# Expert weights loaded as 8 KB runs, and the latents' expert products of the first layer cut into 32-column tiles

## The chip, the cores and the metric

The kernel runs on one core of one Trainium2 chip. The metric is the device time of one launch in microseconds (us), as the median over several runs. The profile is one execution of the same program, recorded instruction by instruction. Engines are named as in the profile: PE (matrix multiply), PEld (its weight load), DVE (vector), ACT (scalar), POOL (GpSimd), SP (the queue that issues most transfers).

## The reference, cut to what matters

The program is two transformer blocks after each other, each of two layers, on 512 latent tokens of width 1024; the second block also carries 256 context tokens. The change touches only the mixture of experts that ends each layer of the second block. In layer 0 it runs on the context and on the latents, in layer 1 on the latents alone.

```python
def ec_moe(h, w_router, w_gate, w_up, w_down):
    bsz, n_tok, d = h.shape
    cap = EC_CAPACITY * n_tok // N_EXPERTS
    aff = jax.nn.softmax(jnp.einsum('bnd,de->bne', h, w_router).astype(jnp.float32), axis=-1)
    g, idx = lax.top_k(jnp.swapaxes(aff, 1, 2), cap)
    xs = jax.vmap(lambda hb, ib: hb[ib])(h, idx)
    hid = jax.nn.silu(jnp.einsum('becd,edf->becf', xs, w_gate)) * jnp.einsum('becd,edf->becf', xs, w_up)
    ye = jnp.einsum('becf,efd->becd', hid, w_down) * g[..., None].astype(h.dtype)
    return jax.vmap(lambda yb, ib: jnp.zeros((n_tok, d), h.dtype).at[ib.reshape(-1)].add(yb.reshape(-1, d)))(ye, idx)
```

There are 16 experts; each takes 64 latent tokens and 32 context tokens (`cap`). Its three weight matrices are 1024 x 1024 in fp32, 4 MB each, so a layer's experts are 192 MB. `h` is the layer-normed token, scaled and shifted by two rows of the conditioning vector (`adaln`).

## The kernel before

`moe(l, lat, ctx_)` works in groups. In layer 0 (`two` is true) there are four groups of four experts, in layer 1 eight groups of two. A group has blocks of 128 gathered token rows: in layer 0 one context block (four experts of 32 tokens) and two latent blocks (two experts of 64 tokens), in layer 1 one latent block. `gather` fetches the rows, transposes them on PE (`tr` into `ptm`; the rows are `q` in the profile) and writes `xT`, with the scale and shift applied on DVE and ACT.

A product has the tokens as the stationary operand (`xT` or `hid`, 32 or 64 columns) and the weights as the moving one, 512 columns at a time. `tile_position=(0, c0)` puts each expert's tokens into their own columns of the array, so that four matmuls of 32 columns, or two of 64, run at the same time. We call four (or two) such neighbours a set. Each fp32 matmul of the program is two recorded instructions, so a set is passed twice. Accumulators are `pm` (six PSUM banks), evacuated by silu on ACT (gate) and a multiply on DVE (up). The product is transposed again into `hid` (two `ptm` banks), and `w_down` is applied. `Columns.down` scales by the router's weight. In all but the last group of layer 0 the rows then go to memory by indirect adds on POOL (`acc`). Elsewhere a one-hot matrix (`sel`) adds them into the rows kept on chip (`Columns.spread`).

`wload` fetches weights in pieces of 1 MB into rotating slots: 14 in layer 0, 18 in layer 1. A piece is one expert's 512 rows by 512 columns, so a run in memory is 512 columns, 2 KB. The last group's `w_down` of layer 1 uses pieces of 256 columns (1 KB runs). One `product` covers 512 columns; gate, up, gate, up, down, down is the order within a group. Within a product the order `every` goes row by row of the contraction (k) over all blocks; `one_by_one` does one block after the other.

A scheduler decides the final order on each engine. SP issues loads in order, and a load waits for the last matmul that read its slot. In layer 1 the 16th to 18th load are issued by POOL (`LATE`).

Of the kernel before, what the change touches and what calls it, by code (L numbers as in the profile page):

```python
# [8 lines left out]
F32 = mybir.dt.float32  # L9
# [4 lines left out]
AF = mybir.ActivationFunctionType  # L14
# [72 lines left out]
def _build(tc, nc, st, a, out):  # L87
# [59 lines left out]
    def pj():  # L147
        return cur["ps"].tile([128, 512], F32, tag="j", name="pj", bufs=2)
# [10 lines left out]
    def tr(o, i):  # L159
        T.transpose(o, i, ident[: i.shape[0], : i.shape[0]])  # L160
# [14 lines left out]
    with tc.tile_pool(name="vl", bufs=1) as vl:  # L175
# [4 lines left out]
        o = 0  # L180
# [47 lines left out]
    def pin(ins, yes=True):  # L228

        return tc.keep_in_program_order(ins) if yes else ins  # L230
# [170 lines left out]
    z_d = [dr.tile([S, D], F32, name=f"z{l}") for l in range(NL)]  # L401
    mod_d = [dr.tile([2, 6 * D], F32, name=f"mod{l}") for l in range(NL)]
    modc = [con.tile([128, 96], F32, name=f"modc{l}") for l in range(NL)]
    cT = con.tile([128, 8, 32], F32, name="cT")

    def cond():
# [7 lines left out]
    def adaln(l, pool):  # L414

        mr = pool.tile([128, 12, 128], F32, tag="mr", name="mr")
        G.memset(mr, 0.0)
        for g in range(4):
            nc.sync.dma_start(mr[32 * g:32 * g + 2, :, :], bass.AP(
                a["b_mod_2"].tensor, a["b_mod_2"].offset + l * 6 * D + 128 * g, [[0, 2], [512, 12], [1, 128]]))  # L420
        for u in range(12):
            p = pj()
            for kq in range(4):
                w = wraw(a["w_mod_2"][l], 2 * kq, 2, 512 * u, 512)
                for k in range(2):
# [12 lines left out]
        V.tensor_copy(modc[l], p[:, :96])  # L438
        for c in range(2):
            for sc in (1, 4):  # L440
                s0 = 48 * c + 8 * sc
                V.tensor_scalar(modc[l][:, s0:s0 + 8], modc[l][:, s0:s0 + 8], 1.0, None, op0=OP.add)

    def mc(l, c, chunk, k):
        o_ = 48 * c + 8 * chunk + k
        return modc[l][:, o_:o_ + 1]
# [656 lines left out]
    def moe(l, lat, ctx_):  # L1103
# [17 lines left out]
        def pm():  # L1121
            return psm.tile([128, 512], F32, tag="m", name="pm", bufs=6)

        def wload(src, e, c0, n, kh):
            turn[0] = (turn[0] + 1) % len(order_)
            pool = order_[turn[0]]
            w = pool.tile([128, 4, 512], F32, tag="w", name="w", bufs=slots[id(pool)])

            late = len(order_) - LATE[l] <= loads[0] < len(order_)
            loads[0] += 1  # L1130
            w = w[:, :, :n]
            pin((nc.gpsimd if late else nc.sync).dma_start(w, src[l, e, 512 * kh:512 * kh + 512, c0:c0 + n].rearrange(
                "(k p) c -> p k c", p=128)), late)
            return w

        gms = {}
# [14 lines left out]
        def gather(s, i):  # L1151

            r = row4()
            pin(G.indirect_dma_start(out=r, out_offset=None, in_=s["rows"][:],
                                 in_offset=bass.IndirectOffsetOnAxis(ap=s["idx"][:, i:i + 1], axis=0)),
                loads[0] < 20)
            xT = xt(s["nm"])
            for kk in range(2):
                p = ptm()
                for k in range(4):  # L1160
                    tr(p[:, 128 * k:128 * k + 128], r[:, 512 * kk + 128 * k:512 * kk + 128 * k + 128])
                for k in range(4):
                    k_ = 4 * kk + k
                    o, i_, g, b = xT[:, k_, :], p[:, 128 * k:128 * k + 128], mc(l, s["c"], 4, k_), mc(l, s["c"], 3, k_)
                    if k % 2:
                        A.activation(o, i_, AF.Identity, bias=b, scale=g)
                    else:
                        V.tensor_scalar(o, i_, g, b, op0=OP.mult, op1=OP.add)  # L1168
            return xT

        def half_tile():
            return small([128, S], "ty", bufs=4)

        def group(i):
# [10 lines left out]
                blocks = [blocks[1], blocks[0], blocks[2]]  # L1185
            exps = [e for p_ in pairs for e in (p_, p_ + 8)]

            def product(src, cols, lhs, order):

                c, n = cols  # L1190
                if order is every:
                    ws = {(e, kh): wload(src, e, c, n, kh) for kh in range(2) for e in exps}
                else:
                    ws = {(e, kh): wload(src, e, c, n, kh) for p_ in pairs for kh in range(2) for e in (p_, p_ + 8)}
                outs = [pm() for _ in blocks]
                for step in order:
                    if callable(step):
                        step(outs)
                        continue
                    bs, ks = step  # L1200
                    for k in ks:
                        for bi in bs:
                            for e, c0, m in blocks[bi][1]:
                                mm(outs[bi][c0:c0 + m, :n], lhs[bi][:, k, c0:c0 + m], ws[e, k // 4][:, k % 4, :],
                                   k == 0, k == 7, tile_position=(0, c0))
                return outs

            all_k = range(8)
# [1 line left out]
            one_by_one = [([b], all_k) for b in range(len(blocks))]  # L1210
            hid = [mB.tile([128, 8, 128], F32, tag=f"hid{j}", name="hid", bufs=1) if two else
                   row4().rearrange("p (a b) -> p a b", b=128) for j in range(len(blocks))]
            for half in range(2):
                order = one_by_one if i == 0 and half == 0 else every
                gp = product(a["w_gate_2"], (512 * half, 512), [b[0] for b in blocks], order)
                gs = []
                for g in gp:
                    x = half_tile()
                    A.activation(x, g, AF.Silu)  # L1219
                    gs.append(x)  # L1220
                up = product(a["w_up_2"], (512 * half, 512), [b[0] for b in blocks], order)
                for bi, u in enumerate(up):
                    V.tensor_tensor(out=gs[bi], in0=u, in1=gs[bi], op=OP.mult)  # L1223
                    p = ptm()
                    for k in range(4):
                        tr(p[:, 128 * k:128 * k + 128], gs[bi][:, 128 * k:128 * k + 128])
                    copy(hid[bi][:, 4 * half:4 * half + 4, :].rearrange("p a b -> p (a b)"), p)

            if i == 0:
                late_rows()  # L1230
# [78 lines left out]
                    self.seen.add(nm)  # L1309

            waiting = None
            for c, n in ((0, 256), (256, 256), (512, 256), (768, 256)) if final and not two else ((0, 512), (512, 512)):
                x = Columns(c, n)
                if final and two:
                    product(a["w_down_2"], (c, n), hid, [
                        ([0], all_k), lambda dp: x.down(0, dp), ([1, 2], range(4)), ([1], range(4, 8)),
                        lambda dp: x.down(1, dp), lambda dp: x.spread(0), ([2], range(4, 6)), lambda dp: x.spread(1),
                        ([2], range(6, 8)), lambda dp: x.down(2, dp), lambda dp: x.spread(2)])
                    continue
                dp = product(a["w_down_2"], (c, n), hid, one_by_one if final else every)  # L1320
# [445 lines left out]
```

## Time and profile before

| What | Value |
|---|---|
| Median of three runs | 2866.74 us (2864.62 to 2875.64) |
| The profiled execution's own time | 2861.59 us |
| Its span, first to last instruction | 2859.8 us |
| PE busy, share of the span | 2483.4 us, 87% |
| Moved by DMA | 612.94 MB, 214 GB/s over the span |

The table is to be read with care: the shares are means over stages that have different limits. Experts of layer 0 run from about 1298 to 1939 us of the span, those of layer 1 from about 2338 us to the end.

### The profile page before, as it was taken

The page shows a single profiled execution, that of the slowest core. Times are in us where ns is not written, and L with a number is a line of the kernel's source. Part 1 is how long each engine was busy: PE and PEld are TensorE (multiplying, and loading weights), DVE is VectorE, ACT ScalarE, POOL GpSimd, SP SyncE. Part 2 cuts the span into 40 slices and gives each one's busy share as a digit, 9 for nine tenths or more (in the row PEclk, how much of TensorE's full clock was granted, in tenths as well). Part 3 has the DMA queues.
Part 4 walks back from the last instruction along what each step waited for, and adds up shares of the span by engine and source line. Part 5 has one row for each costly group of instructions (what it writes and reads, how often), then busy time and mean ns, then how long its engine had stood idle before and what let it go on. Part 6 is the DMA issues. An engine that isn't in the chain of part 4 may idle for free.

```text
span 2859.8 us, 36332 instructions
## 1 busy us (share of the span) xinstructions
PE 2483.4 (87%) x14703; PEld 1412.3 (49%) x14703; DVE 1228.3 (43%) x2361; ACT 802.2 (28%) x1522; POOL 504.6 (18%) x389
## 2 busy tenths in 40 slices
PE   7988898998998878968999999995898869877886
PEld 5755676665687566753222222234677733323233
DVE  5423554335649968762010101028678641212113
ACT  3362323353335436521000000004247320000001
POOL 2111312012223332331010101004223320000001
PEclk9999999999999988988999999997999979999998
DMA  5364553346433141169999998963221479999997
GB/s 183 104 195 126 163 146 110 123 131 186 143 112 132 55 152 36 45 232 326 342 354 340 330 355 297 340 234 104 66 66 37 147 267 387 387 387 387 387 387 272
DMA packets 354191, 612.94 MB, mean 214 GB/s; under 512 B 37585, under 2 KB 110823, under 8 KB 354023
## 3 DMA queue, kind: packets, MB, share of 16 engines
q1 hardware_dynamic: 344214, 576.71, 58.4%
q0 software_dynamic: 5824, 20.45, 2.3%
q10 hardware_dynamic: 3984, 13.45, 1.2%
q8 instruction: 116, 1.90, 0.3%
q14 instruction: 53, 0.43, 0.0%
HBM read 581.88 MB, written 28.67 MB: 213 GB/s over the span
## 4 chain that ended last, share of the span: by engine, by line
PE 39%; DVE 11%; DMA 9%; issue 7%; ACT 3%; POOL 2%; SPq 0%; DVEq 0%; POOLq 0%; ACTq 0%
PE pm L151 24%; PE pj L151 6%; DMA w<-in_w_up_dram 5%; PE pa L151 5%; DMA w<-in_w_down_dram 3%; DVE acc L850 2%; PE pt L151 2%; PE pt L160 1%; DVE wl L331 1%; PE ptm L160 1%; POOL lnst L249 1%; DVE s L245 1%; ACT P L456 1%; DVE Q L1609 0%; DVE ng L453 0%
## 5 line engine op out<-in xcount | busy, mean ns | idle before, releaser
L151 PE MATMUL pm<-w,q 128*64 128x512 f32 (+1 forms) x1600 | 368.9, 583 | 56.2 <-DMA w<-in_w_up_dram 23.0
L151 PE MATMUL pm<-w,xT 128*64 128x512 f32 (+1 forms) x2048 | 389.4, 607 | 0.4 <-DVE xT L1168 0.3
L151 PEld LDWEIGHTS pm<-w,q 128*64 128x64 f32 x1600 | 124.8, 137 | 276.5 <-issue 174.7
L329 ACT ACTIVATE wh<-w 128x1024 fp32r<-128x1024 f32 (+2 forms) x154 | 161.0, 1050 | 303.4 <-PE pj L151 103.4
L1223 DVE TENSOR_TENSOR ty<-pm,ty 128x512 f32<-128x512 f32 x40 | 27.6, 691 | 502.9 <-PE pm L151 502.9
L151 PEld LDWEIGHTS pm<-w,xT 128*64 128x64 f32 (+1 forms) x2048 | 90.5, 123 | 281.1 <-issue 264.7
L151 PE MATMUL pj<-hTh,wh 128*128 128x512 f32 x512 | 214.4, 420 | 12.2 <-ACT ty L301 6.4
L331 POOL TENSOR_TENSOR wl<-w,wh 128x1024 fp32r<-128x1024 f32 (+1 forms) x57 | 142.4, 2500 | 436.6 <-ACT wh L329 403.9
L151 PE MATMUL pm<-w,hid 128*64 128x512 f32 (+1 forms) x1024 | 210.7, 604 | 0.0
L151 PE MATMUL pj<-hTl,wh 128*128 128x512 f32 x512 | 207.7, 406 | 0.0
L151 PE MATMUL pj<-hTh,wl 128*128 128x512 f32 x512 | 205.1, 404 | 0.0
L331 DVE TENSOR_TENSOR wl<-w,wh 128x1024 fp32r<-128x1024 f32 (+2 forms) x97 | 136.3, 1405 | 104.0 <-ACT wh L329 103.6
L160 PE MATMUL pt<-ident,P 128*128 128x128 f32 x712 | 120.5, 289 | 11.2 <-DVE mx L133 3.1
L151 PE MATMUL pa<-wh,hTh 128*128 128x512 f32 x256 | 106.2, 416 | 23.2 <-DVE ty L948 15.1
L151 PEld LDWEIGHTS pm<-w,hid 128*64 128x64 f32 (+1 forms) x1024 | 47.1, 122 | 154.6 <-issue 152.2
L151 PEld LDWEIGHTS pj<-hTh,wh 128*128 128x128 f32 x512 | 100.2, 196 | 38.9 <-issue 8.1
L1219 ACT ACTIVATE ty<-pm 128x512 f32<-128x512 f32 x40 | 23.9, 597 | 314.6 <-PE pm L151 314.6
L151 PEld LDWEIGHTS pj<-hTl,wh 128*128 128x128 f32 x512 | 99.8, 195 | 24.1 <-issue 3.9
L151 PEld LDWEIGHTS pj<-hTh,wl 128*128 128x128 f32 x512 | 98.7, 193 | 24.4 <-issue 2.2
L135 DVE TENSOR_SCALAR P<-P,rc 128x256 f32<-128x256 f32 (+6 forms) x176 | 107.8, 635 | 4.4
L453 DVE TENSOR_REDUCE ng<-pa 128x1 f32<-128x513 f32 (+5 forms) x124 | 93.3, 756 | 36.9 <-PE pa L151 35.0
L151 PE MATMUL pa<-wh,hTl 128*128 128x512 f32 x256 | 104.4, 412 | 1.1 <-DVE hTl L370 1.1
(441 smaller groups left out, 4332.7 us busy)
## 6 DMA issues: line engine op xcount, KB each, us to landing
w<-in_w_gate_dram SPq DMA_DIRECT2D x128, 1024.0 KB
w<-in_w_up_dram SPq DMA_DIRECT2D x127, 1024.0 KB
w<-in_w_down_dram SPq DMA_DIRECT2D x118, 1024.0 KB
w<-in_w_mod_dram SPq DMA_DIRECT2D x96, 512.0 KB
w<-in_w_in_dram SPq DMA_DIRECT2D x94, 512.0 KB
w<-in_w_out_dram SPq DMA_DIRECT2D x40, 512.0 KB
w<-in_w_down_dram SPq DMA_DIRECT2D x16, 512.0 KB
z<-q ACTq DMA_DIRECT2D x8, 512.0 KB
```

The lines of the kernel that those rows point to most:

```text
L135: (G if eng == "g" else V).tensor_scalar(o, i, scale, None, op0=OP.mult)
L151: return T.matmul(o, l, r, start=start, stop=stop_, skip_group_check=True, **kw)
L160: T.transpose(o, i, ident[: i.shape[0], : i.shape[0]])
L245: pin(V.bn_stats(s6[:, c, :], x[:, c * w:c * w + w]))
L249: pin(G.tensor_tensor(out=rs, in0=ve, in1=mhalf[:, :n], op=OP.pow))
L329: A.activation(hi, w, AF.Copy)
L331: (lo_eng or (G if lot[0] % 3 == 0 else V)).tensor_tensor(out=lo, in0=w, in1=hi.bitcast(F32), op=OP.subtract)
L453: V.tensor_reduce(ng, S_[:, :, lo:hi], axis=AX, op=OP.max, negate=True)
L456: A.activation(P[:, i, lo:hi], S_[:, i, lo:hi], AF.Exp, bias=ng[:, i:i + 1], accum_out=su[:, i:i + 1])
L850: V.scalar_tensor_tensor(acc[:, c, :n], glu[:, c, tap:tap + n], w, acc[:, c, :n], op0=OP.mult, op1=OP.add)
L1219: A.activation(x, g, AF.Silu)
L1223: V.tensor_tensor(out=gs[bi], in0=u, in1=gs[bi], op=OP.mult)
```

## The change

Gate and up of every group, and down of all but each layer's last group, use a new function `wide`, with a new loader `wwide`. A piece is again 1 MB, but it is 256 rows by all 1024 columns. Partition p reads rows 4p+m (m is 0, 1 or 2, 3) of one half of the matrix, two neighbouring rows, so one run is 8 KB. Both column halves of a product accumulate at the same time: two `pm` banks for each block, all six in layer 0. Since a partition now holds rows 4p+m, the transposes that make `xT` and `hid` take every fourth column (`wide_rows`). For the same reason scale and shift are fetched in that order into `modw` (two more small transfers and eight small transposes per layer in `adaln`). Silu's output is kept in one `t4` tile per block in layer 0. In layer 0 the latents' blocks are cut into four tiles of 32 columns, two for each expert, in all products. The first group's gate does three quarters of the context block before the latents. The last group's down keeps its old loads.

```diff
+    def wide_rows(x, k):
+        return x[:, 512 * (k // 4):512 * (k // 4) + 512].rearrange("p (j m) -> p m j", m=4)[:, k % 4, :]
...
+        def wwide(src, e, j):
+            w = wslot().rearrange("p (k c) -> p k c", k=2)
             late = len(order_) - LATE[l] <= loads[0] < len(order_)
             loads[0] += 1
+            m = 2 * (j % 2)
+            pin((nc.gpsimd if late else nc.sync).dma_start(
+                w, src[l, e].rearrange("(h p m) c -> p h m c", h=2, m=4)[:, j // 2, m:m + 2, :]), late)
             return w
...
-                    tr(p[:, 128 * k:128 * k + 128], r[:, 512 * kk + 128 * k:512 * kk + 128 * k + 128])
+                    tr(p[:, 128 * k:128 * k + 128], wide_rows(r, 4 * kk + k))
...
+            tiles = [[(e, c, 32) for e, c0, m in b[1] for c in range(c0, c0 + m, 32)] if two else b[1] for b in blocks]
...
+            def wide(src, lhs, early=False):
+                ws = {(e, j): wwide(src, e, j) for j in range(4) for e in exps}
+                outs = {}
+                for b in (rest_ + lats if early else lats + rest_):
+                    outs[b] = pm(), pm()
+                steps = [(b, j) for j in range(4) for b in lats + rest_]
+                if early:
+                    first = [(b, j) for j in range(3) for b in rest_]
+                    steps = first + [x for x in steps if x not in first]
+                for b, j in steps:
+                    for k in (2 * j, 2 * j + 1):
+                        for h in range(2):
+                            for e, c0, m in tiles[b]:
+                                mm(outs[b][h][c0:c0 + m, :], lhs[b][:, k, c0:c0 + m],
+                                   ws[e, j][:, k % 2, 512 * h:512 * h + 512], k == 0, k == 7, tile_position=(0, c0))
                 return outs
...
-            for half in range(2):
-                order = one_by_one if i == 0 and half == 0 else every
-                gp = product(a["w_gate_2"], (512 * half, 512), [b[0] for b in blocks], order)
...
+            gp = wide(a["w_gate_2"], xTs, two and i == 0)
...
+            up = wide(a["w_up_2"], xTs)
...
+            if not final:
+                dw = wide(a["w_down_2"], hid)
```

PE, layer 0, the start of the second group's gate, before (`xT` names the stationary tokens, `q` with its number the gathered rows of one latent block; the counts are matmuls of the program):

```order
L160 MATMUL ptm<-ident,q_11667 128x128 x4
L151 MATMUL pm<-w,xT 64x512 x2
L151 MATMUL pm<-w,xT 32x512 x3
L151 MATMUL pm<-w,xT 64x512 x2
L151 MATMUL pm<-w,xT 32x512
L151 MATMUL pm<-w,xT 64x512 x14
L151 MATMUL pm<-w,xT 32x512 x3
L151 MATMUL pm<-w,xT 64x512 x4
L151 MATMUL pm<-w,xT 32x512 x4
L151 MATMUL pm<-w,xT 64x512 x4
```

From here the rows alternate between four matmuls of 32 and four of 64 columns through the group, with sets broken in places as at the top. The same place on PE after the change, through gate and up into down (numbers behind `q` differ for the two latent blocks and the context):

```order
L160 MATMUL ptm<-ident,q_11844 128x128 x8
L160 MATMUL ptm<-ident,q_11865 128x128 x8
L151 MATMUL pm<-w,xT 32x512 x27
L160 MATMUL ptm<-ident,q_11886 128x128 x8
L151 MATMUL pm<-w,xT 32x512 x357
L160 MATMUL ptm<-ident,q_12140 128x128 x8
L160 MATMUL ptm<-ident,q_12143 128x128 x4
L151 MATMUL pm<-w,hid 32x512 x13
L160 MATMUL ptm<-ident,q_12143 128x128 x4
L151 MATMUL pm<-w,hid 32x512 x2
L160 MATMUL ptm<-ident,q_12146 128x128 x4
L151 MATMUL pm<-w,hid 32x512 x16
```

Another four transposes and 161 matmuls of 32 columns end the group. The 64-column tiles are gone, gate and up stand as one stretch, and the transposes for `hid` stand together between up and down.

PE, layer 1, one group in the middle, before (`q_17498` are the gathered rows, `q_17500` is xT, `q_17519` hid, `ty` with `sel` the spread into the rows kept on chip):

```order
L160 MATMUL ptm<-ident,q_17498 128x128 x8
L151 MATMUL pm<-w,q_17500 64x512 x40
L160 MATMUL ptm<-ident,ty 128x128 x4
L151 MATMUL pm<-w,q_17500 64x512 x24
L151 MATMUL pm<-w,q_17519 64x512
L160 MATMUL ptm<-ident,ty 128x128 x4
L151 MATMUL pm<-w,q_17519 64x512 x15
L151 MATMUL pm<-ty,sel 128x512 x4
L151 MATMUL pm<-w,q_17519 64x512
L151 MATMUL pm<-ty,sel 128x512 x4
L151 MATMUL pm<-w,q_17519 64x512 x15
L151 MATMUL pm<-ty,sel 128x512 x8
```

And one group after, where `q_18050` is xT and `q_18069` hid:

```order
L160 MATMUL ptm<-ident,q_18048 128x128 x8
L151 MATMUL pm<-w,q_18050 64x512 x64
L160 MATMUL ptm<-ident,ty 128x128 x8
L151 MATMUL pm<-w,q_18069 64x512 x32
L151 MATMUL pm<-ty,sel 128x512 x16
```

Matmuls, transposes and spreads are as many as before, but none of the transposes or spreads stands between two products any more.

SP's queue at the start of layer 1's experts, before:

```order
L1132 DMA w<-in_w_gate_dram 128x4x512 x4
L1132 DMA w<-in_w_up_dram 128x4x512 x4
L1132 DMA w<-in_w_gate_dram 128x4x512 x4
L1132 DMA w<-in_w_up_dram 128x4x512 x3
L1132 DMA w<-in_w_down_dram 128x4x512 x6
```

and after:

```order
L1158 DMA w<-in_w_gate_dram 128x2048 x8
L1158 DMA w<-in_w_up_dram 128x2048 x7
L1158 DMA w<-in_w_down_dram 128x2048 x6
L1158 DMA w<-in_w_gate_dram 128x2048 x8
L1158 DMA w<-in_w_up_dram 128x2048 x8
```

As many loads of the same size stand there (three more of this group are POOL's); each is now 128 runs of 2048 elements where it was 512 runs of 512.

## Rows read from the trace of the kernel before

**Rows 1.** Busy time by stage; us, PE, PEld, DVE, ACT, POOL, PEclk, DMA share, GB/s.

```profile
1298.00:1448.00 150.00, 149.29 (x828) 41.30 (x832) 17.21 (x32) 13.12 (x24) 5.93 (x8) 0.98 0.97 349
1448.00:1606.00 158.00, 157.82 (x820) 38.79 (x816) 15.45 (x28) 10.70 (x22) 13.97 (x12) 1.00 0.96 339
1606.00:1769.00 163.00, 163.00 (x808) 38.88 (x800) 13.65 (x24) 10.41 (x21) 13.32 (x11) 1.00 0.93 329
1769.00:1939.00 170.00, 164.28 (x855) 46.46 (x852) 32.15 (x58) 15.59 (x29) 9.68 (x8) 0.99 0.79 277
1939.00:2338.00 399.00, 308.41 (x1955) 245.14 (x1954) 298.89 (x581) 167.62 (x301) 135.58 (x97) 0.88 0.32 105
2350.00:2805.00 455.00, 378.58 (x1627) 141.42 (x1623) 83.86 (x142) 33.75 (x65) 5.68 (x6) 1.00 1.04 387
2805.00:2859.80 54.80, 30.76 (x202) 17.03 (x202) 25.95 (x50) 6.97 (x12) 7.64 (x3) 0.86 0.70 237
```

**Rows 2.** Waits of PE, 1300 to 1938: total us, times, longest.

```profile
PE pm L151 <- ACT ty L1272: 4.0, 1, 4.0
PE ptm L160 <- ACT xT L1166: 1.7, 1, 1.7
```

**Rows 3.** Waits of SP's queue, 1300 to 1938.

```profile
SPq L1132 <- PE pm L151: 466.9, 91, 34.2
```

**Rows 4.** Busy time in stretches of layer 0: mixed, 32-column only, 64-column only.

```profile
1475.95:1498.85 22.90, 22.90 (x132) 5.13 (x128) 2.07 (x3) 0.00 (x0) 0.61 (x1) 1.00 1.04 383
1327.82:1334.82 7.00, 7.00 (x65) 1.98 (x64) 0.00 (x0) 0.60 (x1) 0.00 (x0) 1.00 1.04 387
1334.82:1348.71 13.89, 13.89 (x69) 4.51 (x65) 1.38 (x2) 0.00 (x0) 0.00 (x0) 1.00 1.03 371
```

**Rows 5.** Timeline of PE, 1605 to 1612: start, us, instructions merged.

```profile
1605.72 2.78 PE L151 MATMUL pm<-w,xT 128*32 128x512 f32 x24 [0.18 <-DVE xT L1168]
1608.43 0.66 PE L160 MATMUL ptm<-ident,q 128*128 128x128 f32 x4
1609.02 1.06 PE L151 MATMUL pm<-w,xT 128*32 128x512 f32 x8
```

**Rows 6.** Weight loads of the transposes, by line, 1180 to 1900.

```profile
L160 PEld LDWEIGHTS ptm<-ident,q 128*128 128x128 f32 x96 | 10.9, 147 | 18.3 <-issue 8.6 <-ACT xT L1166 4.4 <-DMA q<-rowsc,idx 2.9
```

**Rows 7.** DMA totals, 2811:2824 (1 KB runs), 2360:2380 (2 KB), 1873:1879 (4 KB).

```profile
DMA packets 4546, 4.53 MB, mean 348 GB/s; under 512 B 141, under 2 KB 4545, under 8 KB 4545
...
DMA packets 3905, 7.74 MB, mean 387 GB/s; under 512 B 127, under 2 KB 127, under 8 KB 3905
...
DMA packets 676, 2.47 MB, mean 411 GB/s; under 512 B 71, under 2 KB 71, under 8 KB 676
```

**Rows 8.** The page's DMA queues: packets, MB, share of 16 engines.

```profile
q8 instruction: 116, 1.90, 0.3%
```

**Rows 9.** The chain that ended last, from 2330: shares, then pieces.

```profile
by line: PE pm L151 42.6%; DMA w<-in_w_up_dram 28.3%; DMA w<-in_w_down_dram 15.4%; DVE ty L1263 2.0%; ACT ty L1272 1.6%; SPq L1132 1.6%; PE ptm L160 1.1%; DVE q L1302 0.9%; DVE q L1359 0.8%; DMA q<-rowsl,idx 0.8%; issue 0.7%; DVE q L1356 0.
...
2442.45 1.44 PE pm L151 x5
...
2459.55 14.37 DMA w<-in_w_up_dram
...
2508.16 15.82 DMA w<-in_w_up_dram
```

**Rows 10.** Waits of PE, 2340 to 2810.

```profile
PE pm L151 <- DMA w<-in_w_up_dram: 21.4, 17, 1.6
PE pm L151 <- ACT ty L1272: 20.6, 14, 1.6
```

**Rows 11.** Groups by line, 2442 to 2508, one group of layer 1.

```profile
L151 PE MATMUL pm<-w,q 128*64 128x512 f32 x192 | 46.6, 598 | 8.2 <-DMA w<-in_w_up_dram 3.3 <-DMA w<-in_w_down_dram 1.8 <-DVE q L1168 1.8
...
L1273 DVE TENSOR_TENSOR ty<-ty 128x512 fp32r<-128x512 f32 x3 | 2.1, 692 | 2.2 <-ACT ty L1272 2.2
L1272 ACT ACTIVATE ty<-ty 128x512 fp32r<-128x512 f32 x3 | 1.9, 629 | 31.2 <-DVE ty L1263 31.2
...
L1263 DVE SCALAR_TENSOR_TENSOR ty<-pm,gat,gm 128x512 f32<-128x512 f32 x2 | 1.5, 751 | 15.3 <-PE pm L151 15.3
...
L1223 DVE TENSOR_TENSOR ty<-pm,ty 128x512 f32<-128x512 f32 x2 | 1.4, 691 | 28.0 <-PE pm L151 28.0
```

More of the change, by code (lines that the diff above doesn't have):

```diff
@@ L403, in _build @@
     modc = [con.tile([128, 96], F32, name=f"modc{l}") for l in range(NL)]
+    modw = [con.tile([128, 8, 4], F32, name=f"modw{l}") for l in range(NL)]
     cT = con.tile([128, 8, 32], F32, name="cT")
@@ L442, in adaln @@
                 V.tensor_scalar(modc[l][:, s0:s0 + 8], modc[l][:, s0:s0 + 8], 1.0, None, op0=OP.add)
+        mrow = mr[0:4, 0:8, :].rearrange("p a b -> p (a b)")
+        for c in range(2):
+            nc.sync.dma_start(mrow[2 * c:2 * c + 2, :], mod_d[l][c, 3 * D:5 * D].rearrange("(a d) -> a d", a=2))
+        p = pj()
+        for k in range(8):
+            tr(p[:, 4 * k:4 * k + 4], wide_rows(mrow, k))
+        V.tensor_copy(modw[l].rearrange("p k c -> p (k c)"), p[:, :32])
+        for c in range(2):
+            V.tensor_scalar(modw[l][:, :, 2 * c + 1], modw[l][:, :, 2 * c + 1], 1.0, None, op0=OP.add)
+    def wide_rows(x, k):
+        return x[:, 512 * (k // 4):512 * (k // 4) + 512].rearrange("p (j m) -> p m j", m=4)[:, k % 4, :]
     def mc(l, c, chunk, k):
@@ L1122, in pm, with wslot, wload @@
             return psm.tile([128, 512], F32, tag="m", name="pm", bufs=6)
[L1124 removed]
+        def wslot():
             turn[0] = (turn[0] + 1) % len(order_)
             pool = order_[turn[0]]
[L1127 removed]
+            return pool.tile([128, 2048], F32, tag="w", name="w", bufs=slots[id(pool)])
+        def wload(src, e, c0, n, kh):
+            w = wslot().rearrange("p (k c) -> p k c", k=4)[:, :, :n]
+            loads[0] += 1
+            nc.sync.dma_start(w, src[l, e, 512 * kh:512 * kh + 512, c0:c0 + n].rearrange("(k p) c -> p k c", p=128))
+            return w
+        def wwide(src, e, j):
+            w = wslot().rearrange("p (k c) -> p k c", k=2)
             late = len(order_) - LATE[l] <= loads[0] < len(order_)
             loads[0] += 1
[L1131 to L1133 removed]
+            m = 2 * (j % 2)
+            pin((nc.gpsimd if late else nc.sync).dma_start(
+                w, src[l, e].rearrange("(h p m) c -> p h m c", h=2, m=4)[:, j // 2, m:m + 2, :]), late)
             return w
@@ L1160, in gather @@
                 for k in range(4):
-                    tr(p[:, 128 * k:128 * k + 128], r[:, 512 * kk + 128 * k:512 * kk + 128 * k + 128])
+                    tr(p[:, 128 * k:128 * k + 128], wide_rows(r, 4 * kk + k))
                 for k in range(4):
                     k_ = 4 * kk + k
-                    o, i_, g, b = xT[:, k_, :], p[:, 128 * k:128 * k + 128], mc(l, s["c"], 4, k_), mc(l, s["c"], 3, k_)
+                    b, g = (modw[l][:, k_, 2 * s["c"] + j:2 * s["c"] + j + 1] for j in range(2))
+                    o, i_ = xT[:, k_, :], p[:, 128 * k:128 * k + 128]
                     if k % 2:
@@ L1202, in product @@
                         for bi in bs:
-                            for e, c0, m in blocks[bi][1]:
+                            for e, c0, m in tiles[bi]:
                                 mm(outs[bi][c0:c0 + m, :n], lhs[bi][:, k, c0:c0 + m], ws[e, k // 4][:, k % 4, :],
                                    k == 0, k == 7, tile_position=(0, c0))
+                return outs
+            lats = [b for b, x in enumerate(blocks) if x[2] is lat]
+            rest_ = [b for b, x in enumerate(blocks) if x[2] is not lat]
+            def wide(src, lhs, early=False):
[13 more added lines that the diff above has]
+                                   ws[e, j][:, k % 2, 512 * h:512 * h + 512], k == 0, k == 7, tile_position=(0, c0))
                 return outs
@@ L1212, in group @@
                    row4().rearrange("p (a b) -> p a b", b=128) for j in range(len(blocks))]
-            for half in range(2):
-                order = one_by_one if i == 0 and half == 0 else every
-                gp = product(a["w_gate_2"], (512 * half, 512), [b[0] for b in blocks], order)
[L1216 to L1223, printed above, removed]
+            xTs = [b[0] for b in blocks]
+            gp = wide(a["w_gate_2"], xTs, two and i == 0)
+            gs = {}
+            for b in gp:
+                gs[b] = t4() if two else None
+                for h in range(2):
+                    x = gs[b][:, h, :] if two else half_tile()
+                    A.activation(x, gp[b][h], AF.Silu)
+                    gp[b] = gp[b][:h] + (x,) + gp[b][h + 1:]
+            up = wide(a["w_up_2"], xTs)
+            for b in up:
+                for h in range(2):
+                    x = gp[b][h]
+                    V.tensor_tensor(out=x, in0=up[b][h], in1=x, op=OP.mult)
                     p = ptm()
                     for k in range(4):
-                        tr(p[:, 128 * k:128 * k + 128], gs[bi][:, 128 * k:128 * k + 128])
-                    copy(hid[bi][:, 4 * half:4 * half + 4, :].rearrange("p a b -> p (a b)"), p)
+                        tr(p[:, 128 * k:128 * k + 128], x[:, 128 * k:128 * k + 128] if final else
+                           x.rearrange("p (j m) -> p m j", m=4)[:, k, :])
+                    copy(hid[b][:, 4 * h:4 * h + 4, :].rearrange("p a b -> p (a b)"), p)
             if i == 0:
@@ L1319, in group @@
                     continue
-                dp = product(a["w_down_2"], (c, n), hid, one_by_one if final else every)
+                dp = product(a["w_down_2"], (c, n), hid, one_by_one) if final else {b: dw[b][c // 512] for b in dw}
                 for bi in range(len(blocks)):
```

## Prediction

> **What bounds the kernel now.** I read the busy time by stage first. The experts of layer 0 fill four stretches of 150, 158, 163 and 170 us, one for each group, and those of layer 1 one stretch up to the end [rows 1]. In layer 0 PE is busy all the time at a granted clock of 1.00 (0.98 in the first group), while DMA moves 277 to 349 GB/s, less than the 387 that it reaches later. The waits agree: PE waited 5.7 us in two places over 640 us [rows 2], and the load queue stood 466.9 us waiting for PE to free a slot [rows 3]. So layer 0 is PE's. In layer 1, from 2350 to 2805, DMA holds 387 GB/s without a break and PE is busy 379 of 455 us [rows 1]. The chain runs through weight loads there: 28.3% `w_up` and 15.4% `w_down`, in pieces of 14 to 16 us [rows 9]. PE's own waits are short and many [rows 10]; in such a stretch the bytes decide. What lies between the two layers (1939 to 2338) is not touched.
>
> **Part 1: the array's tiles in layer 0.** A full product is eight rows of k, each one context set of four and two latent sets of two, every set passed twice: 48 passes. A stretch of exactly one product's worth takes 22.90 us, 0.477 us a pass. Sixteen passes of 32-column tiles alone take 7.00 us (0.438), thirty-two of 64-column tiles alone 13.89 us (0.434) [rows 4]. So four tiles of 32 cost no more than two of 64, and what a mixed row pays beside that is the change of tile width, twice in each k. The two pure stretches each hold one such edge; their difference, 6.89 us for 16 more passes, gives 0.431 without it. With one width throughout, a product is 48 x 0.431 = 20.7 us, 2.2 us less; six products make 13.2 us a group.
>
> [...]
>
> Next, broken sets. The second group took 158 us. Six products at 22.9 are 137.4. A batch of four transposes costs 0.59 us from its start to the next matmul, and the six passes ahead of it 2.71 us where 6 x 0.431 is 2.59 [rows 5], so 0.71; twelve batches are 8.5 us. With no waits, the remaining 12 us are sets that the order splits, as the rows of the order before show (three and one, two and two). After the change the order splits sets at x27, x13, x2 and x16: four extra sets of two passes, 3.5 us. So 8.5 us more are saved.
>
> Transposes are as many as before. They stand in longer runs, but there are two `ptm` banks, so a third batch waits for the evacuation of the first: I add 1.5 us a group. A middle group is then 48 x 6 x 0.431 = 124.1, plus 8.5, 3.5 and 1.5: 137.6 us. Against 158 and 163 that is -20 and -25. The first group keeps its slow start (some 2.5 us), 140 against 150: -10. The last group has four wide products (-8.8), and its down, which was already less mixed, loses some splits (-5): -14. Layer 0: **-69 us**.
>
> **Part 2: strided transposes.** `wide_rows` makes PE load every fourth column as the stationary operand, in 168 transposes of layer 0 and 120 of layer 1. No row shows a strided load. A contiguous one is busy 10.9/96 = 0.114 us and hides beside the matmul of the one before [rows 6]. Bounds: nothing, if the stride is free; doubled, +0.114 x 168 = +19 us in layer 0; fourfold, +57. I take **+8**, nearer to nothing, since only the stride differs from the contiguous row. In layer 1 it hides behind the loads.
>
> **Part 3: runs of 8 KB.** Rates in saturated stretches are 348 GB/s at 1 KB, 387 at 2 KB and 411 at 4 KB [rows 7]. For one of 16 engines that is 47, 85 and 159 ns a packet: 37.5 ns for each KB and 9.6 fixed. An 8 KB packet would take 310 ns, 423 GB/s (my extrapolation). Layer 1's saturated stretch moves 455 x 387 = 176 MB; at 423 it takes 416 us (-39), at 411 428 us (-27), and at an unchanged rate nothing is gained. I take **-34**, nearer to the trend of three rows. Its end (1 KB runs, last spread, norms) is as before.
>
> PE must keep up. A group of layer 1 is 96 passes of two, 41.4 us, with 16 transposes (2.4) and 16 spread matmuls (3.8 to 5). Now that the halves are not interleaved, PE stands after up for the multiply and copy (0.69 each), after down for scaling, rounding and difference (0.75, 0.63, 0.69) [rows 11], and for xT, some 6 us together: 54 us. Loads need (24 x 1.05 + 0.5) MB / 423 = 61 us, so the stalls lie behind DMA.
>
> In layer 0 the loads must follow PE as well: 158 x 339 = 53.6 MB a group [rows 1] take 130 us at 411 and 127 at 423, under 137.6; at 387 138.5. At the start 14 slots are full, and none is freed until three quarters of the context and one of each latent block are through, some 17 us. Gate has 24 us of work left then and four pieces come in 10 us, so I cost it at nothing; the lead is thin, and without it the first group is late by what is missing, at most these 17 us.
>
> All six banks of layer 0 are held by one product. Silu (two of 0.6 us for a block) has 7 us of other blocks' matmuls to hide behind. The indirect adds have the next group's gate. **Part 4:** `modw` costs two small transfers, eight transposes and three vector operations per layer, beside other work: **+1**.
>
> **The sum** on the profiled execution: 2861.6 - 69 + 8 - 34 + 1 = 2767.6. The median of the runs is 5.1 us above that execution, so 2772.7; I say 2772. With the bounds of parts 2 and 3 and some 12 us for waits that I may have misjudged, this case runs from 2747 to 2792.
>
> **Rivals.** (a) Long runs bring nothing and loads stay at 387. For it: no row shows 8 KB from the load queue. Layer 1 then stands still, and layer 0's groups are paced by loads at about 139 to 141: -57, 2810. (b) The strided loads cost fourfold: +57 in place of +8, and layer 1's PE comes to 54 + 16 x 0.34 = 59 us a group, just under the loads at 61, so that some 5 us of the gain there go: -40, 2827. [...] (c) Layer 1's PE chain without the interleaving is longer than my 54 us, and above 66 nothing is gained there: -60, 2807. For it: PE already waited 20.6 us for the rounding on ACT [rows 10]. Against it: 12 us more in each group would have to be found.
> (d) Slower: long runs are served at a lower rate. For it: the only packets of 8 KB and more in the trace, the instruction fetch, took 0.3% of 16 engines' span for 116 packets, 1.2 us each, about 14 GB/s an engine against 24 at 2 KB [rows 8]; these come one at a time, which speaks against it, as does the trend of rows 7. Below about 360 GB/s it decides: layer 1 is 34 us longer there, and layer 0's groups are paced at 149. At 340 layer 1 takes 518 us (+63) and layer 0's groups 158, no gain: 2930.
>
> **Chances.** Forecast 0.63; (a) 0.10; (b) 0.08; (c) 0.11; (d) 0.06; no change for a reason not seen 0.02. All but (d) and the last are faster by over 0.5%, 0.92; within 0.5% (about what a measurement of this kernel can tell from none) 0.03; slower 0.05. The range takes in (a), (b), (c) and the better end of the forecast: 2740 to 2832.
>
> **What would show it.** Right: the middle groups of layer 0 at about 138 us with PE busy throughout, passes 0.43 us apart without the 64-column rows; layer 1's saturated stretch above 410 GB/s and about 420 us long. Part 2 shows in the weight loads of `ptm` and in batches longer than 0.6 us. Wrong: PE in layer 0 waiting for `w_gate` or `w_up`; the rate at 387 or below; in layer 1, PE busy or waiting for DVE and ACT while DMA has gaps.

## The result and the profile after

The changed kernel takes 2773.39 us (median of four runs, 2767.23 to 2777.70) against 2865.68 for the kernel before, run beside it: 0.967, 95% interval 0.964 to 0.970. The profiled execution took 2777.7 us (span 2775.9), the longest of the four, while the profiled one of before, 2861.59, was shorter than all four of its kernel here; between the two traces lie 83.9 us, between the medians 92.3. One of e11's five runs below took 2908.80 us at a granted clock of 0.82 (the others 0.94) and is left out of its median and ratio.

Busy time by stage after the change: the four groups of layer 0, the saturated part of layer 1 and its end (columns as in [rows 1]).

```profile
1314.00:1456.30 142.30, 137.77 (x1209) 47.19 (x1209) 17.54 (x34) 13.28 (x27) 6.22 (x7) 0.98 0.93 374
1456.30:1596.50 140.20, 135.98 (x1201) 44.20 (x1201) 14.77 (x27) 10.46 (x22) 13.90 (x12) 0.99 0.98 384
1596.50:1736.80 140.30, 136.04 (x1201) 47.12 (x1201) 14.75 (x27) 10.51 (x22) 13.88 (x12) 0.99 0.97 381
1736.80:1883.30 146.50, 146.07 (x1224) 48.47 (x1224) 25.00 (x43) 12.28 (x23) 8.27 (x7) 0.99 0.85 316
...
2305.00:2705.00 400.00, 345.45 (x1502) 131.96 (x1500) 81.88 (x140) 31.50 (x62) 5.65 (x6) 0.95 1.01 421
2705.00:2775.90 70.90, 50.56 (x294) 24.94 (x294) 27.09 (x52) 8.17 (x14) 7.63 (x3) 0.86 0.66 237
```

The middle groups take 140 us where they took 158 and 163, and DMA moves 421 GB/s in layer 1 where it moved 387 [rows 1]. The first stage does not start at 1298 any more, but at 1314. PE is no longer busy throughout in layer 0: 4.2 us are missing in each middle group. The waits of PE there (total us, times, longest), to be held against [rows 2]:

```profile
PE ptm L160 <- ACT xT L1193: 11.8, 3, 3.9
```

The place is the end of a group; PE's timeline (start, us) shows eight transposes, a hole, eight more, and then the next gate:

```profile
1451.11 1.23 PE L160 MATMUL ptm<-ident,q 128*128 128x128 f32 x8
1456.27 1.71 PE L160 MATMUL ptm<-ident,q 128*128 128x128 f32 x8 [3.92 <-ACT xT L1193]
1457.90 7.31 PE L151 MATMUL pm<-w,xT 128*32 128x512 f32 x54
```

DVE's timeline at the same place says why. Its six scalings of down (L1318) begin only as PE ends its last product, and stand ahead of the first `xT`:

```profile
1450.36 4.04 DVE L1318 SCALAR_TENSOR_TENSOR q<-pm,gat,gm 128x512 f32<-128x512 f32 x6 [38.01 <-PE pm L151]
1454.32 0.72 DVE L1195 TENSOR_SCALAR xT<-ptm,modw 128x128 f32<-128x128 f32 x2
```

ACT, which the waits name, only comes after DVE on the same `xT`, at 1454.82. Both `ptm` banks are full until then.

In layer 1 the chain that ended last runs through loads as before, now 57.9% of it, in pieces of 20 us (start, us):

```profile
by line: PE pm L151 34.6%; DMA w<-in_w_up_dram 25.3%; DMA w<-in_w_gate_dram 20.3%; DMA w<-in_w_down_dram 12.3%; DVE q L1416 0.9%; PE ptm L160 0.9%; DVE q L1357 0.8%; DVE q L1413 0.7%; DVE s L1361 0.5%; DVE ty L1276 0.4%; issue 0.4%; DVE q L
...
2522.64 19.81 DMA w<-in_w_down_dram
2542.51 19.91 DMA w<-in_w_gate_dram
2562.49 21.10 DMA w<-in_w_up_dram
```

So layer 1 is still bound by its bytes, at a higher rate.

### The profile page after: what moved, and what is told of

Same layout as the page of the kernel before. It is cut to its first block, busy times and chain, and to the rows that moved or that the text cites. A ratio compares the mean times of both kernels' runs of the same rounds, so it can differ in the third digit from the quotient of the medians.

```text
span 2775.9 us, 39464 instructions
## 1 busy us (share of the span) xinstructions
PE 2406.4 (87%) x16255; PEld 1439.1 (52%) x16255; DVE 1224.7 (44%) x2367; ACT 801.2 (29%) x1522; POOL 508.8 (18%) x389
## 4 chain that ended last, share of the span: by engine, by line
PE 35%; DVE 13%; DMA 11%; issue 8%; ACT 2%; POOL 2%; DVEq 0%; POOLq 0%; ACTq 0%; SPq 0%
PE pm L151 20%; PE pj L151 5%; PE pa L151 5%; DMA w<-in_w_up_dram 4%; DMA w<-in_w_gate_dram 4%; DVE acc L865 3%; DMA w<-in_w_down_dram 2%; PE pt L151 2%; PE pt L160 1%; DVE wl L331 1%; PE ptm L160 1%; DVE s L245 1%; POOL lnst L249 1%; ACT P L471 1%; DVE ng L468 1%
## 5 line engine op out<-in xcount | busy, mean ns | idle before, releaser
L151 PE MATMUL pm<-w,q 128*64 128x512 f32 (+1 forms) x1600 | 359.5, 597 | 40.3 <-DMA w<-in_w_up_dram 27.6
L151 PE MATMUL pm<-w,xT 128*32 128x512 f32 x3072 | 338.7, 599 | 0.0
L151 PEld LDWEIGHTS pm<-w,xT 128*32 128x32 f32 x3072 | 104.4, 111 | 228.1 <-issue 223.6
L151 PE MATMUL pm<-w,hid 128*32 128x512 f32 x1536 | 178.5, 593 | 0.0
L1276 DVE TENSOR_TENSOR q<-pm,q 128x512 f32<-128x512 f32 x24 | 16.6, 692 | 285.6 <-PE pm L151 285.6
L1276 DVE TENSOR_TENSOR ty<-pm,ty 128x512 f32<-128x512 f32 x16 | 11.1, 691 | 256.4 <-PE pm L151 256.4
L1180 POOL DMA_INDIRECT q<-rowsl,idx x16 | 15.4, 960 | 563.0 <-PE ptm L160 432.7
L151 PEld LDWEIGHTS pm<-w,hid 128*32 128x32 f32 x1536 | 50.4, 110 | 112.5 <-issue 110.7
L865 DVE SCALAR_TENSOR_TENSOR acc<-glu,vec,acc 128x512 f32<-128x512 f32 x120 | 108.6, 946 | 0.1
```

Source lines behind the costliest of these rows:

```text
L151: return T.matmul(o, l, r, start=start, stop=stop_, skip_group_check=True, **kw)
L865: V.scalar_tensor_tensor(acc[:, c, :n], glu[:, c, tap:tap + n], w, acc[:, c, :n], op0=OP.mult, op1=OP.add)
L1276: V.tensor_tensor(out=x, in0=up[b][h], in1=x, op=OP.mult)
```

## The experiments

All times below are us. "Start" is the first transpose for `xT` of layer 0; "layer 0" goes from there to its last matmul with weights; "layer 1" from its first such transpose to the end of the span. These are read from the one profiled execution of each kernel; median and ratio (to the kernel before on the same chip, with its 95% interval) from its runs.

| Kernel | Start | Layer 0 | Between | Layer 1 | Median | Ratio |
|---|---|---|---|---|---|---|
| before | 1298.5 | 633.9 | 404.1 | 523.2 | 2865.68 | 1 |
| after | 1314.2 | 569.1 | 400.7 | 491.9 | 2773.39 | 0.967 (0.964-0.970) |
| e1_tiles64 | 1303.8 | 592.5 | 396.8 | 491.3 | 2786.91 | 0.974 (0.972-0.976) |
| e2_runs2k | 1305.9 | 580.3 | 400.1 | 528.4 | 2813.97 | 0.983 (0.981-0.985) |
| e3_runs4k | 1303.2 | 584.9 | 398.6 | 513.2 | 2802.53 | 0.979 (0.978-0.981) |
| e4_contiguous | 1310.4 | 565.6 | 401.2 | 492.7 | 2767.93 | 0.967 (0.965-0.968) |
| e5_after_again | 1312.7 | 569.1 | 403.3 | 491.9 | 2774.42 | 0.968 (0.966-0.970) |
| e6_no_modw | 1296.9 | 569.3 | 395.1 | 490.5 | 2756.15 | 0.963 (0.961-0.965) |
| e7_before_tiles32 | 1301.3 | 564.4 | 398.9 | 522.9 | 2790.08 | 0.975 (0.973-0.976) |
| e8_down_by_block | 1305.8 | 588.3 | 395.4 | 492.0 | 2782.65 | 0.971 (0.969-0.973) |
| e9_modw_on_pe | 1296.9 | 569.1 | 394.8 | 490.6 | 2761.56 | 0.965 (0.964-0.967) |
| e10_best_of_both | 1300.6 | 562.3 | 395.3 | 490.3 | 2750.22 | 0.962 (0.960-0.963) |
| e11_rows_ahead | 1302.7 | 563.9 | 405.3 | 492.3 | 2767.21 | 0.967 (0.966-0.969) |
| e12_no_transfers | 1306.8 | 569.2 | 395.6 | 490.5 | 2767.26 | 0.968 (0.965-0.970) |

The stages of one kernel's two profiles (after, e5) agree to 0.1 us in both layers, while "between" varies by 10 us over kernels that don't differ there. So the two layers are compared by their columns, the start by the means of several profiles, and the rest by medians.

### The tiles: e1 and e7

```diff
# e1, from the changed kernel
-            tiles = [[(e, c, 32) for e, c0, m in b[1] for c in range(c0, c0 + m, 32)] if two else b[1] for b in blocks]
+            tiles = [b[1] for b in blocks]
# e7, from the kernel before
+            tiles = [[(e, c, 32) for e, c0, m in b[1] for c in range(c0, c0 + m, 32)] if two else b[1] for b in blocks]
...
-                            for e, c0, m in blocks[bi][1]:
+                            for e, c0, m in tiles[bi]:
```

> The changed kernel with the latents' tiles of layer 0 left at 64 columns; loads, order of the rows and transposes as changed. Theory E (a tile itself costs the same, only the changes of width cost, 0.1375 us each by 2.2 us over 16 in a product of before): the wide product does four pieces of k in a row of blocks, so two column halves together change width 8 times, not 32; a group of layer 0 has 24 changes more than with 32 columns, 3.3 us, and the kernel comes 13 us (with the last group's down up to 20) above the changed kernel's median of 2773, so 2786 to 2793. Theory P (cutting the latents into 32 columns is what pays, 13 us a group as the prediction's sum has it): 2820 or more. [...]

> The kernel before with nothing but the latents' tiles of layer 0 cut into 32 columns; loads, halves and transposes as before. Theory E (16 changes of width gone in each product, 2.2 us, and broken sets mended): groups of 158 and 163 go to 138 to 141, where loads at 387 GB/s pace them (53.6 MB in 138.5 us); layer 0 50 to 60 us shorter, layer 1 unchanged: 0.979 to 0.983 of before. Rival (the sets' cutting does little by itself, and what layer 0 gained came from both column halves at once): 0.995 or above.

In e1 a middle group took 143.4, 3.1 more than after, for the 3.3 of theory E; its last group took far more. Windows of its third and fourth group:

```profile
1593.40:1736.80 143.40, 139.06 (x819) 45.34 (x818) 14.76 (x27) 10.48 (x22) 13.84 (x11) 0.99 0.95 373
1736.80:1895.70 158.90, 158.90 (x828) 48.65 (x828) 23.37 (x38) 11.64 (x22) 8.12 (x6) 1.00 0.78 287
```

The last is 12.4 longer than its match after, with PE busy all the time: in its down, sets of 64 and of 32 columns alternate in broken pieces (in the trace three matmuls of 32, one of 64, one of 32, one of 64, and so on), and I put the 12.4 down to them. So layer 0 lost 23.4, not the 13 to 20 expected. In the median this was partly made up by a start 10.4 earlier, and 2787, inside the 2786 to 2793 forecast, was met by luck.

e7 is the surprise. With that one line the kernel before loses 69.5 us in layer 0, more than the whole change did there (64.8). Windows of e7's four groups:

```profile
1301.30:1437.70 136.40, 136.37 (x1199) 43.13 (x1200) 15.19 (x28) 12.51 (x23) 3.61 (x5) 0.98 1.01 372
1437.70:1574.10 136.40, 136.26 (x1202) 44.12 (x1200) 15.45 (x27) 10.68 (x21) 13.92 (x11) 1.00 1.05 380
1574.10:1715.10 141.00, 139.16 (x1212) 45.45 (x1208) 17.84 (x32) 11.38 (x23) 16.04 (x13) 1.00 1.05 380
1715.10:1865.80 150.70, 148.45 (x1224) 49.23 (x1224) 25.76 (x45) 12.82 (x25) 8.68 (x7) 1.00 0.93 335
```

PE has hardly a hole at a group's end (0.1 us in the second group): DVE scales down in two threes there, at 1552.67 while PE multiplies the other column half, and at 1573.27. The loads at 2 KB just suffice, 380 GB/s at a DMA share of 1.05. My expectation had them pace the groups at 138.5 and was 9 us too careful. The rival falls: the tiles alone give layer 0 its whole gain, and the rest of the change (long runs, both halves at once, strided transposes) took 4.7 us of it back, 3.5 of them the stride's (e4). The parts overlap, though: without the tiles the rest still brings layer 0 41.4 us (633.9 to 592.5, e1), since both halves at once also leave fewer changes of width and fewer broken sets (in the second group's trace 95 changes and 318 passes before, 24 and 294 in e1, none and 298 in e7).

### The run length: e2 and e3

```diff
# e2: 512 rows by 512 columns again, four neighbouring rows a partition
+            c = 512 * (j % 2)
...
-                w, src[l, e].rearrange("(h p m) c -> p h m c", h=2, m=4)[:, j // 2, m:m + 2, :]), late)
+                w, src[l, e].rearrange("(h p m) c -> p h m c", h=2, m=4)[:, j // 2, :, c:c + 512]), late)
...
# e3: rows two apart
-                w, src[l, e].rearrange("(h p m) c -> p h m c", h=2, m=4)[:, j // 2, m:m + 2, :]), late)
+                w, src[l, e].rearrange("(h p m) c -> p h m c", h=2, m=4)[:, j // 2, j % 2::2, :]), late)
...
```

> The changed kernel with the same bytes in each piece, but a piece is 512 rows by 512 columns again, four neighbouring rows for each partition, so runs of 2 KB; transposes, tiles, both column halves at once and the evacuations as changed. Theory L (the run length sets the rate, and the rate sets layer 1): 387 GB/s in layer 1's saturated stretch, +36 to +39 us there; layer 0's groups need 138.5 us of loads and take 140 now, so 0 to +8: 2809 to 2820. Rival O (layer 1 became shorter because transposes and spreads no longer stand between the products): 2773 to 2780, whatever the rate.

> The changed kernel with the same pieces of 256 rows by 1024 columns, but each partition takes rows two apart, so runs of 4 KB; nothing else differs but the order of the rows of k. Theory L: 411 GB/s in layer 1's saturated stretch, +9 to +12 us there and nothing in layer 0: 2782 to 2786. Rival O: 2773. A third theory (a step in memory between the two runs costs as much as short runs): 2809 or more.

DMA totals from 2360 to 2700 us, first the changed kernel, then e2, then e3:

```profile
DMA packets 19994, 143.08 MB, mean 421 GB/s; under 512 B 2219, under 2 KB 2219, under 8 KB 2859
```

```profile
DMA packets 65580, 131.59 MB, mean 387 GB/s; under 512 B 2044, under 2 KB 2044, under 8 KB 65568
```

```profile
DMA packets 35920, 138.48 MB, mean 407 GB/s; under 512 B 2147, under 2 KB 2147, under 8 KB 35906
```

At 387 layer 1 takes 36.5 longer, with transposes and spreads grouped as after the change: rival O falls, the rate is all of layer 1's gain. e3 missed its forecast by some 18. Its rate is 407, not 411, and layer 1 takes 21.3 more. The rate makes some 14 of these; most of the rest lies in its first two stretches of 50 us, at 373 and 399 GB/s where the changed kernel moved 401 and 421, and why they are slower was not tried. Layer 0 took 15.8 more, where I had expected nothing: PE waited for `w_gate` there, as in e2. Waits of PE in layer 0, e2 and then e3:

```profile
PE pm L151 <- DMA w<-in_w_gate_dram: 11.9, 5, 4.2
```

```profile
PE pm L151 <- DMA w<-in_w_gate_dram: 9.1, 3, 5.3
```

So with both halves at once layer 0 needs the long runs; with one half after the other (e7) 2 KB did. That this comes from the slots, which are freed in another rhythm, was not tried.

### The strided transposes: e4

```diff
-                    tr(p[:, 128 * k:128 * k + 128], wide_rows(r, 4 * kk + k))
+                    tr(p[:, 128 * k:128 * k + 128], r[:, 512 * kk + 128 * k:512 * kk + 128 * k + 128])
```

The same was done for `hid`.

> The changed kernel with the transposes for xT and hid taking 128 neighbouring columns again (so that tokens meet the wrong rows of the weights; all else is done). Theory S (the stride costs 0.06 us a weight load, of which 0.01 to 0.1 shows): layer 0 shorter by 4 to 8 us, layer 1 unchanged behind its loads: 2765 to 2769. Rival F (free): 2773. Rival Q (the fourfold price of the prediction's rival): 2716.

Weight loads of the transposes from 1180 to 1880 us, the changed kernel and then e4:

```profile
L160 PEld LDWEIGHTS ptm<-ident,q 128*128 128x128 f32 x192 | 26.7, 203 | 37.7 <-issue 14.3 <-ACT xT L1193 12.3 <-DVE q L1276 3.4
```

```profile
L160 PEld LDWEIGHTS ptm<-ident,q 128*128 128x128 f32 x192 | 22.7, 152 | 38.9 <-issue 14.2 <-ACT xT L1193 12.9 <-DVE q L1276 3.4
```

The mean is 51 ns longer. As 24 of the 192 loads are the last group's, not strided, it's some 58 ns for each of the 168 that are. Of that 3.5 us show in layer 0 (0.02 each), nothing in layer 1. The stride is neither free nor fourfold; theory S holds, with 3.5 just under its 4 to 8.

### The late start: e5, e6, e9, e12

```diff
# e9: modw from the rows that already lie on chip
+        for b in range(4):
+            for m in range(4):
+                mm(p[32 * b:32 * b + 32, 8 * m:8 * m + 8], mraw.rearrange("r (q m) -> r m q", m=4)[:, m, :],
+                   ident[:96, :96].rearrange("p (c g b) -> p b c g", c=2, b=4)[:, b, :, 6:10], True, True,
+                   tile_position=(0, 32 * b))
...
# e12
-        for c in range(2):
-            nc.sync.dma_start(mrow[2 * c:2 * c + 2, :], mod_d[l][c, 3 * D:5 * D].rearrange("(a d) -> a d", a=2))
```

> The changed kernel as it is, a second time, beside the others of this call. Theory V (the first transposes of layer 0's experts came 15.7 us later than before by the spread from run to run): they stand between 1303 and 1310 us here, as in the experiments before, which have the same code ahead of the experts, and the median is 0.967 of before's, 2767 where before has 2861. Theory M (modw delays them): again 1314.

> The changed kernel without modw: no additional transfers, transposes or vector operations in adaln; scale and shift are taken from the columns of before, which stand in another order than the rows (so that tokens get others' scale). Theory M: layer 0's first transposes at 1298 to 1300 us, the kernel shorter by 4 to 15 us than the run of the changed kernel beside it. Theory V: first transposes at 1303 to 1310 as with modw, within 2 us of the run beside it. The prediction's own price for modw is 1 us.

> The changed kernel with modw made by 16 small matmuls from the rows of the conditioning vector that already lie on chip, in place of two transfers and eight transposes for each layer; all else as changed. Theory D (the transfers, and the buffer that they hold longer, which delays the next layer's loads of the bias, cost the start of layer 0's experts some 9 us and more): first transposes at 1297 to 1301 us as without modw, 0.963 to 0.964 of before. Rival (any modw in adaln shifts the order of what stands around it): 1303 to 1314 and 0.967 to 0.968 as with the transfers.

> The changed kernel without the two small transfers of modw in each layer; its eight transposes and three vector operations stay and read what the buffer of the rows holds (so that scale and shift are other numbers). The buffer is held as long as in the changed kernel, so layer 1's bias loads stand as late in the load queue (behind eight loads more than before). Theory H (the late bias loads and the transposes cost the 8.5 us at the start of layer 0's experts): first transposes at 1303 to 1314 us and 0.967 to 0.969 of before. Theory T (the two transfers themselves, each with a wait for memory, cost it): 1297 to 1301 us, 0.963 to 0.965.

Theory V falls. The nine profiles with `modw` as changed (e12 among them, without its transfers) start at 1302.7 to 1314.2, mean 1307.3; the five without it or with it on PE (before, e6, e7, e9, e10) at 1296.9 to 1301.3, mean 1298.8. That is 8.5 us. The medians say more: beside each other on one chip e6 was 18 faster than e5, where I had expected 4 to 15. Their two profiles lie 25.1 apart, 15.8 at the start and 8.2 in "between". The transfers aren't the cause: without them e12 starts at 1306.8 and takes 0.968. e9's early start is weak evidence: that profile is the shortest of its five runs, 8.4 below their median, and the median's ratio, 0.965, lies between what theory D and the rival gave. What e12 keeps and e9 has not are the eight transposes, 1.12 us a layer, and `mr`, the buffer that is held for them. Layer 1's bias loads into it stand at 404.9 us in place of 356.0, behind ten other transfers in place of one. SP's timeline in the changed kernel, then in e9:

```profile
360.85 10.19 SPq L321 DMA_DIRECT2D w<-in_w_out_dram  x4
...
404.90 2.94 SPq L420 DMA_DIRECT2D mr<-in_b_mod_dram  x4
```

```profile
355.37 0.39 SPq L321 DMA_DIRECT2D w<-in_w_out_dram  x1
356.04 1.28 SPq L420 DMA_DIRECT2D mr<-in_b_mod_dram  x4
```

and SP waits behind them there: waits up to 800 us in the changed kernel, in e9 and in e12.

```profile
SPq L321 <- DMA mr<-in_b_mod_dram: 9.5, 2, 8.2
```

```profile
SPq L321 <- DMA mr<-in_b_mod_dram: 2.4, 2, 1.5
```

```profile
SPq L321 <- DMA mr<-in_b_mod_dram: 9.4, 3, 7.1
```

But these 7 us don't reach PE as they stand. In the traces the nine are behind the five, in the mean, by 0.6 us at the first of SP's 96 loads of `w_mod` (some 87 us), by 2.5 at the 65th (some 566), by 5.1 at the last (some 740) and by 8.0 at the last load of `w_out` ahead of the experts (some 1220). So most of the delay builds up long after that wait. What makes it, the held buffer, the transposes or the order of other work, which shifts as well, stays open; the start varies by 11 us among kernels with the same code there.

### The hole at a group's end: e8 and e11

```diff
# e8
...
+            for b in lats + rest_:
+                for x in cols:
+                    x.down(b, {b: dw[b][x.c // 512]})
...
# e11 besides, ahead of down
+            if two and not final:
+                fetch(ctx_, i + 1)
+                for j in range(npair):
+                    fetch(lat, npair * (i + 1) + j)
```

> The changed kernel with down's scalings given in the order in which the blocks end (both column halves of the one latent block, of the other, then of the context), not the context's first; the same operations otherwise. Theory W (at the end of a group of layer 0 the vector engine's first scaling waits for the context, the last to end, and all six stand in a row behind it, ahead of the next group's xT, for which PE waits 3.9 us): four of six are done before, PE waits 1.3 us or less, three groups by 2.6 us or more: 8 to 12 us shorter than the changed kernel beside it. Rival (PE waits there for the gathered rows or for ACT anyway): within 2 us.

> The changed kernel with down's scalings in the order in which the blocks end, as in the earlier run, and the next group's gathered rows fetched before down, so that they don't stand behind the indirect adds on POOL. Theory W (PE's 3.9 us at each group's end are the vector engine's queue): middle groups 136.5 to 138 in place of 140.3, layer 0's experts 558 to 563 in place of 569; 0.963 to 0.965 of before with modw as it is. Rival (another wait takes its place, as the gathered rows did): 140 or more.

e8 was to save 8 to 12 us and cost 19.2 us in layer 0. PE's timeline at the same place, then POOL's:

```profile
1449.45 1.95 PE L160 MATMUL ptm<-ident,q 128*128 128x128 f32 x8 [6.84 <-DMA q<-rowsc,idx]
1453.22 1.96 PE L160 MATMUL ptm<-ident,q 128*128 128x128 f32 x8 [1.82 <-DMA q<-rowsl,idx]
```

```profile
1436.82 1.54 POOL L1395 DMA_INDIRECT accl<-q,idxe  x1 [130.73 <-DVE q L1318]
1438.66 1.04 POOL L1180 DMA_INDIRECT q<-rowsc,idx  x1 [0.31 <-PE pm L151]
```

The wait for `xT` is gone, but the scheduler put the first indirect add ahead of the next group's gathers, and POOL stood 130.73 us at that add until its rows were scaled. In e11 the gathers come first: groups of 138.7, 136.4 and 140.4 us (from gate to gate) and 145.9 to the end, where the changed kernel has 141.8, 140.4, 140.3 and 144.1. PE's waits for `xT` in layer 0 (11.8 in all after the change), and the end of the third group:

```profile
PE ptm L160 <- ACT xT L1202: 4.6, 3, 1.6
```

```profile
1708.84 0.39 PE L160 MATMUL ptm<-ident,q 128*128 128x128 f32 x1
1709.15 7.06 PE L151 MATMUL pm<-w,hid 128*32 128x512 f32 x44
```

So each wait is 1.5 or 1.6 in place of 3.9, which bears out theory W for the most part. The second group is 4.0 shorter, more than that wait; in the third, the order puts a single transpose among down's matmuls, which breaks sets (the 44 behind it take 7.06 us, the 78 ahead of it 9.28), and takes the gain away. Layer 0 as a whole is 5.2 shorter, a little less than the 6 to 11 expected; in the median, 0.967 and not the 0.963 to 0.965 expected, nothing can be told against other runs of the changed kernel.

### Both: e10

e10 is e7's layer 0 with the changed layer 1, and `modw` for layer 1 alone as in e9.

> Layer 0 as in the kernel before with nothing but the latents' tiles cut into 32 columns (one column half after the other, runs of 2 KB, contiguous transposes); layer 1 as changed (runs of 8 KB, both halves at once, strided transposes), with modw for layer 1 alone and from 16 small matmuls. If the parts add: start 1297 to 1303, layer 0's experts 564, between 395 to 403, layer 1 491: 2747 to 2761, 0.960 to 0.964 of before. If layer 0's loads at 387 GB/s, late at its end, or the modw still cost what they did in the changed kernel: 2770 or more.

The parts add: 2750.22, 0.962 of before, below the changed kernel's interval. Its second group and its layer 1:

```profile
1436.90:1573.30 136.40, 136.26 (x1201) 44.12 (x1200) 15.45 (x28) 10.65 (x21) 13.90 (x11) 1.00 1.05 379
...
2280.00:2680.00 400.00, 347.05 (x1498) 132.23 (x1496) 81.88 (x140) 31.48 (x61) 5.66 (x6) 0.95 1.01 421
```

## Why the prediction was right

**Part 1** held in size: layer 0 lost 64.8 where -69 and the +8 of part 2 gave -61. Its prices held as well. A pass cost 0.43 us in tiles of 32 (e7), as in the pure stretches of [rows 4]. 24 changes of width cost 3.1 us (e1), 0.13 each, where I had 2.2/16. Counted in the traces, the second group made 95 changes and 318 passes before, none and 294 after; at these prices that is 12 and 10 us, where I had 13.2 and 8.5. Two things were off. The third batch of transposes, costed at 1.5 us, stands 3.9 us at each group's end, since all six accumulators end together; so 140.3 and not 137.6, and PE was not busy throughout. And I did not see that both halves at once bring layer 0 nothing on top of the tiles: the tiles alone did more (e7). The loads' price at 387 GB/s, 138.5 us a group, was too dear: e7 took 136.4 with 2 KB runs.

**Part 2**, +8, is 3.5 (e4), and rival (b) with its fourfold price is out: a load takes 203 ns for 152 in the mean. The factor of four was an assumption of mine, which no run shows.

**Part 3** was right in mechanism and size. The extrapolated 423 GB/s is 421, and layer 1 lost 31.3 of the 34; e2 gives 36.5 for the rate alone. That excludes rivals (a) and (d). For (c): PE waits some 26 us for DVE and ACT in layer 1, but DMA has no gap at 421.

**Part 4** is the term that was mis-sized: +1, measured 8.5 at the start in the mean of the profiles, and more by the medians of e5 and e6. I counted the instructions of `modw`, some 1 us of transposes a layer, and nothing that they hold up: the buffer `mr` and the loads behind its next ones. That these are the cause is not shown (e12, and the lag above).

**The sum** for the profiled execution, 2767.6, was 10.1 too low against 2777.7. Part 4 makes 7.5 of it, part 3 2.7 and part 1 0.7, part 2 takes back 4.5; this execution's start is 7.2 later than the mean of its kind, and "between" 3.4 shorter than before. That the median met the forecast to 1.4 us is partly luck: parts 4 and 3 fell short by 10.2, part 2 and a shorter "between", which the prediction took as untouched, gave 7.9 back.

## What to carry to other kernels

Where column tiles of two widths alternate on PE, count the changes of width first: here one line that made them equal was worth more than the rest of the change together in that stage (69.5 us against 41.4). Look at which accumulators end at the same moment: what evacuates them stands ahead of the next group's work on that engine, and when that is mended, at the next queue (here POOL's adds ahead of the gathers). The price of a small addition is not only its own instructions (here some 8 us for about 1 us a layer): look at what stands behind it in the queues, and measure it by a kernel without it.

## What the runs showed of the hardware

Loads from the queue ran at 387, 407 and 421 GB/s with runs of 2, 4 and 8 KB, for the same pieces of 1 MB (e2, e3, after); the 4 KB runs of e3, with a gap between two runs, were below the 411 of [rows 7]. Four column tiles of 32 took the same pass of 0.43 us as two of 64 (e7, [rows 4]), and a change of width some 0.13 us (e1). Loads of a stationary operand, most of them of every fourth fp32 column, took 203 ns in the mean in place of 152, of which some 20 ns a load showed (e4). PE's granted clock in layer 1's saturated stretch was 0.95, where it had been 1.00 [rows 1], while PE was busy 345 of 400 us. This isn't the rate: in e2, at the 387 GB/s of before, it was lower still.

```profile
2386.00:2436.00 50.00, 37.52 (x148) 13.26 (x146) 8.81 (x17) 4.08 (x8) 0.94 (x1) 0.83 1.04 387
```

PE's longest wait for `w_up` there was 1.6 us before [rows 10], 5.2 after and 9.7 in e3; that the longer waits lower the clock was not tried. Behind the loads it cost nothing that the runs show.
